# Two-layer decoder trunk on one core: queries in reversed order without the copied bias table, scores of two heads in one 128-row matmul over zero-padded keys, value products alternating between heads

## The chip, the cores and the metric

The kernel runs on one core of one Trainium2 chip. The metric is device time in microseconds (us) for one execution. TensorE (PE) does the matmuls, VectorE (DVE) and ScalarE (ACT) do elementwise work and empty the accumulator memory (PSUM), GpSimd (POOL) does elementwise work in SBUF, and SyncE (SP) issues most of the DMAs. Each engine works through its own list of instructions in order and waits for others by semaphores.

## The reference, cut to what matters

The trunk has two layers. Layer 0 runs Mamba-2 heads (SSM) and attention heads beside each other and joins them in one output projection. Layer 1 is a convolution module. Each layer ends with a gated feed-forward part (FFN). The change touches the attention: 16 key/value heads of width 64, and for each of them three queries with three patterns (window and dilation). The bias of a score depends only on the distance between query and key, through a small table.

```python
ATT_PATTERNS = ((128, 1), (512, 4), (2048, 16))

def dilated_branch(q, k, v, bias_tab, window, dil):
    ...
    delta = blk + i - j
    band = (delta >= 0) & (delta <= blk)
    ...
    bias = jnp.transpose(bias_tab[t5_bucket(jnp.maximum(delta, 0) * dil)], (2, 0, 1)).astype(jnp.float32)
    sc = jnp.einsum('bnirhd,bnjrhd->bnrhij', qb, kw).astype(jnp.float32) * (dh ** -0.5) + bias
    sc = jnp.where(mask[None, :, None, None], sc, -jnp.inf)
    m = jnp.max(sc, -1, keepdims=True)
    pr = jnp.exp(sc - m)
    l = jnp.sum(pr, -1, keepdims=True)
    o = jnp.einsum('bnrhij,bnjrhd->bnirhd', (pr / l).astype(v.dtype), vw)
    ...
```

The three patterns of a head are then joined with weights from a softmax over their log-sums. There are 512 tokens.

## The kernel before

All activations lie feature-major (features on the 128 partitions, the 512 tokens along the free axis). Projections with weights run as three passes in a 12-bit split of float32 (`products`, lines 206, 207 and 209): each output tile of 128x512 takes 24 matmuls. `slab` loads up to 2048 weights per partition by SP, casts them on ACT (line 193) and takes the rest on DVE (line 194). A scheduler that ran when the kernel was built placed the instructions in the engines' lists, from the dependences, the buffers of the pools and a cost model; so the order of the source isn't the order of an engine.

The stages that matter here:

- **SSM, four groups.** `ssm_inputs` makes the inputs of a group by `products` (tiles `bc`, `x`, `z`). `ssm_group` walks four chunks of 128 tokens. For each chunk SP loads `ar` (line 485: 512 KB, rows of `a_dram` spread over all partitions) and, from the second chunk on, `ef` (line 512, two DMAs). POOL subtracts in `ar` (486), DVE clips it (487), ACT takes the exponential (488), DVE multiplies by the mask `cb` (498, 499), and PE forms `pd` (503: weights of 64 columns, so a head fills half of the array's columns, and the heads of a chunk take the halves in turn), `po` (515) and `pst` (525). The tiles `ef` and `xde` have two buffers each, and `draw` and `arow` share one.
- **The bias.** Ahead of the groups the bias of all distances is computed into `bv` and written to `b_dram` (16 heads x 896 floats, 56 KB). Four DMAs (line 563) then copy it 128 times over into `b_rep`, 7 MB in DRAM. For the scores of a pair of heads, three DMAs (line 691) fetch `bt` (128 queries x 2 heads x 512 keys) from `b_rep`: partition i reads copy i, and starts i elements earlier than partition 0, since a query one later is one farther from each key. That is the step `LTOT - 1` in the access pattern.
- **Attention, eight pairs of heads.** `att_inputs` makes keys and three queries for two heads at a time (tiles `kq`, `qq`), 64 partitions for each head, and values (`v`, lines 645 to 648) for each second pair. `att_pair` takes one head after the other (`for e in range(2)`): 12 score matmuls over 64 rows, 128 or 256 keys wide (line 707), each emptied by one DVE instruction that adds the bias and takes the maximum (708); exponentials on ACT (732); 11 transposes (745) whose copies are `pt`. After both heads come the 22 value products (lines 788 to 793) with weights of 64 columns, all of head 0 ahead of those of head 1 in the source. The weights of the three patterns go through DRAM (`s_dram`, `w_dram`) and come back as `at`. The outputs of two pairs enter the output projection (`mixed_chunk`); with `y_chunk` and the next pair's `products` it is the work that PE has beside the chain of a pair. Keys `k0` and queries `q0` of the natural order lie in one buffer for even pairs and another for odd ones; `k1`, `q1`, `q2` in the order by token modulo 4 have one buffer.
- **FFN, convolution, FFN, final norm** follow.

Of the kernel before, what the change touches and what calls it, by code (L numbers as in the profile page):

```python
# [9 lines left out]
F32 = mybir.dt.float32  # L10
# [3 lines left out]
ALU = mybir.AluOpType  # L14
# [32 lines left out]
def shape_constants():  # L47
    """Identity, triangle and the buckets of the distances: from shapes alone."""
# [28 lines left out]
def trunk_kernel(ctx: ExitStack, tc, a, out, dbg=None):  # L77
# [14 lines left out]
    # ---------------------------------------------------------------- constants and parameters  # L92
# [7 lines left out]
    def rows(specs, name, col=None):  # L100
        """Vectors as rows of 128, transposed to a column for each row."""
# [16 lines left out]
    def ada_load(pool, l, j0, q, bufs):  # L118
        """Half slabs of ada_w, four chunks of columns wide."""
# [26 lines left out]
    # ---------------------------------------------------------------- adaLN vectors  # L146
# [50 lines left out]
    def products(w, offs, acts, name, tag="pj", cols=ALL, outs=None):  # L197
        """A bank for each list of weight offsets; acts are (hi, lo) pairs."""
# [29 lines left out]
    class Stat:  # L228
        """Sum over features of the squares, for each token of cols."""
# [36 lines left out]
    def spread(v, nb, name):  # L266
        """v [tokens of a block, block] to a bank that holds it in each partition."""
# [13 lines left out]
    class Norm:  # L281
        """h = x * rstd * g * (1 + sc) + sh, feature-major, in two parts."""
# [71 lines left out]
    # ---------------------------------------------------------------- the other parameters  # L354
# [20 lines left out]
    # ---------------------------------------------------------------- SSM  # L375
# [11 lines left out]
    draw = ssm.tile([HEADS, T], F32, tag="draw", name="draw", bufs=1)  # L387
# [44 lines left out]
    arow = ssm.tile([HEADS, T], F32, tag="draw", name="arow", bufs=1)  # L432
# [44 lines left out]
    def ssm_group(g, bt, ct, xs, zs):  # L477
        y1 = ssm.tile([P, 4, T], F32, tag="y1", name=f"y1_{g}", bufs=1)
        prev = None
        for c in range(NB):  # L480
# [37 lines left out]
            if c < NB - 1:  # L518
# [3 lines left out]
                xde = ssm.tile([P, HPG, 64], F32, tag="xde", name="xde" + n)  # L522
# [38 lines left out]
    b_rep = dram.tile([16, P * LTOT], F32, name="b_rep")  # L561
    for q in range(4):
        nc.sync.dma_start(b_rep[4 * q:4 * q + 4, :].rearrange("h (i u) -> h i u", u=LTOT),  # L563
                          b_dram[4 * q:4 * q + 4, :].unsqueeze(1).broadcast_to([4, P, LTOT]))

# [14 lines left out]
    # ---------------------------------------------------------------- attention  # L580
# [7 lines left out]
    SB = "ABABCCCAB"  # L588
# [12 lines left out]
    def out_chunk(rows_, acts, name, last=None, after=None):  # L601
        """Four tiles of wout's rows, by the heads' outputs."""
# [31 lines left out]
    def values(hp):  # L634
        """The values of two pairs of heads, token-major in both orders of the tokens."""
# [18 lines left out]

    def att_inputs(hp, vs):
        def cols(o):
            return (win[:, o + hp * P:o + (hp + 1) * P], KT, P)
# [5 lines left out]
        def nat(tag, ps, scale):  # L663
            t = (att if hp % 2 else early).tile([P, T], F32, tag=tag, name=tag + n, bufs=1)
            S.mul(t, ps, scale) if scale != 1.0 else S.copy(t, ps)
            r[tag] = t

        def mod4(tag, ps, scale):
            t = early.tile([P, 4, P], F32, tag=tag, name=tag + n, bufs=1)
            src = ps.rearrange("p (i r) -> p r i", r=4)  # L670
            S.mul(t, src, scale) if scale != 1.0 else S.copy(t, src)
# [3 lines left out]
        nat("k0", pk, 1.0)  # L675
        mod4("k1", pk, 1.0)
# [8 lines left out]
    def att_pair(hp, r, vs):  # L685
        n = str(hp)
        bt = att.tile([P, 2, T], F32, tag="bt", name="bt" + n, bufs=1)
        bd = b_rep[2 * hp:2 * hp + 1, :]
# [438 lines left out]
```

## Time and profile before

| | us |
|---|---|
| time, median of 3 runs | 1974.75 (1972.83 to 1978.38) |
| span of the profiled execution, first to last instruction | 1970.1 |
| what lies around the span, against the median | 4.65 |
| SSM stage, about | 95 to 455 |
| attention stage, about | 455 to 965 |
| FFN, convolution module, FFN, final norm, about | 965 to 1970 |

The profile comes from one execution and names each instruction by the line of the kernel. A matmul in float32 shows as two records (two passes); the end of a matmul record is modelled, so the step from one record's start to the next one's start tells more than its length. `x8` at the end of a row of the timeline means that eight records stand together. In the tables by stretch, "busy" is the time of an engine with an instruction under way, and PEclk is the share of full speed that TensorE's clock was granted.

### The profile page before, as it was taken

The page shows a single profiled execution, that of the slowest core. Times are in us where ns is not written, and L with a number is a line of the kernel's source. Part 1 is how long each engine was busy: PE and PEld are TensorE (multiplying, and loading weights), DVE is VectorE, ACT ScalarE, POOL GpSimd, SP SyncE. Part 2 cuts the span into 40 slices and gives each one's busy share as a digit, 9 for nine tenths or more (in the row PEclk, how much of TensorE's full clock was granted, in tenths as well). Part 3 has the DMA queues.
Part 4 walks back from the last instruction along what each step waited for, and adds up shares of the span by engine and source line. Part 5 has one row for each costly group of instructions (what it writes and reads, how often), then busy time and mean ns, then how long its engine had stood idle before and what let it go on. Part 6 is the DMA issues. An engine that isn't in the chain of part 4 may idle for free.

```text
span 1970.1 us, 24711 instructions
## 1 busy us (share of the span) xinstructions
PE 1808.6 (92%) x9469; PEld 1493.7 (76%) x9469; DVE 1152.9 (59%) x2164; ACT 753.1 (38%) x1460; POOL 560.2 (28%) x486
## 2 busy tenths in 40 slices
PE   5863788999999999999899999998899999999998
PEld 3642666778687877877888888887779888888888
DVE  7714878666543545554876567348799753333336
ACT  5312323333433444333532122234777542222125
POOL 1413878352242434000300000005897510000001
PEclk8986898999999999998899999998999999999999
DMA  8426454454444444341555555333220332323224
GB/s 296 112 104 188 131 155 133 121 132 129 119 119 108 139 108 140 97 129 55 172 186 199 171 186 183 101 96 119 86 86 1 108 108 85 107 87 106 86 77 138
DMA packets 227842, 246.29 MB, mean 125 GB/s; under 512 B 11770, under 2 KB 195900, under 8 KB 227725
## 3 DMA queue, kind: packets, MB, share of 16 engines
q1 hardware_dynamic: 216589, 202.78, 33.7%
q0 software_dynamic: 11136, 41.95, 6.6%
q8 instruction: 74, 1.21, 0.3%
q14 instruction: 43, 0.35, 0.1%
HBM read 236.06 MB, written 15.98 MB: 128 GB/s over the span
## 4 chain that ended last, share of the span: by engine, by line
PE 68%; DVE 13%; DMA 6%; SPq 4%; ACT 3%; issue 3%; POOL 2%; DVEq 0%; ACTq 0%; POOLq 0%
PE fd L206 4%; PE fd L209 4%; PE fd L207 4%; PE fg L207 4%; PE fu L207 4%; PE fu L206 4%; PE fu L209 4%; PE fg L209 4%; PE fg L206 4%; PE s L707 3%; SPq L563 2%; DMA adap<-in_ada_w 2%; DVE cps L991 2%; PE wa L206 1%; PE qq L206 1%
## 5 line engine op out<-in xcount | busy, mean ns | idle before, releaser
L248 POOL TENSOR_TENSOR n_acc<-n_acc,n_q 128x256 f32<-128x256 f32 x32 | 27.5, 861 | 542.1 <-ACT n_q L244 541.9
L206 PE MATMUL fd<-uh,wd_h 128*128 128x512 f32 (+1 forms) x448 | 150.1, 351 | 0.9 <-DVE xT L596 0.9
L194 DVE TENSOR_TENSOR wf_l<-wf_w,wf_h 128x1024 fp32r<-128x1024 f32 x88 | 106.2, 1243 | 75.4 <-ACT wf_h L193 75.4
L207 PE MATMUL fd<-uh,wd_l 128*128 128x512 f32 (+1 forms) x448 | 147.8, 346 | 0.0
L193 ACT CAST wf_h<-wf_w 128x1024 fp32r<-128x1024 f32 x88 | 87.7, 1048 | 117.5 <-PE fd L209 73.4
L207 PE MATMUL fg<-n_h,wf_l 128*128 128x512 f32 x320 | 125.1, 391 | 2.0 <-DVE wf_l L194 2.0
L206 PE MATMUL fg<-n_h,wf_h 128*128 128x512 f32 x320 | 125.3, 392 | 0.7 <-ACT wf_h L193 0.5
L207 PE MATMUL fu<-n_h,wf_l 128*128 128x512 f32 x320 | 124.7, 390 | 0.0
L206 PE MATMUL fu<-n_h,wf_h 128*128 128x512 f32 x320 | 124.5, 389 | 0.0
L984 POOL TENSOR_TENSOR cv<-cv,pr 128x256 f32<-128x256 f32 x150 | 114.8, 795 | 15.1 <-ACT pr L983 13.0
L732 ACT ACTIVATE s<-s,nm 128x128 f32<-128x128 f32 x192 | 79.6, 416 | 83.8 <-DVE nm L728 53.9
L171 POOL TENSOR_TENSOR adap<-adap 128x512 f32<-128x512 f32 (+2 forms) x96 | 101.7, 1065 | 4.3
L862 DVE TENSOR_TENSOR fs<-fs,fu 128x512 f32<-128x512 f32 x40 | 27.5, 688 | 127.8 <-PE fu L209 127.8
L596 DVE SCALAR_TENSOR_TENSOR xT<-fd,mod,xT 128x512 f32<-128x512 f32 (+1 forms) x64 | 39.1, 616 | 101.5 <-PE fd L209 101.2
L193 ACT CAST wd_h<-wd_w 128x1024 fp32r<-128x1024 f32 (+1 forms) x64 | 57.1, 940 | 103.0 <-PE fd L209 82.8
L206 PEld LDWEIGHTS fd<-uh,wd_h 128*128 128x128 f32 x448 | 84.3, 188 | 13.2 <-DVE xT L596 1.3
L209 PE MATMUL fd<-ul,wd_h 128*128 128x512 f32 (+1 forms) x448 | 93.1, 346 | 0.0
L207 PEld LDWEIGHTS fd<-uh,wd_l 128*128 128x128 f32 x448 | 84.3, 188 | 11.0
L169 POOL TENSOR_TENSOR adap<-adap,cs 128x1024 f32<-128x1024 f32 x32 | 65.5, 2050 | 87.3 <-DMA adap<-in_ada_w 87.3
L194 DVE TENSOR_TENSOR wd_l<-wd_w,wd_h 128x1024 fp32r<-128x1024 f32 (+1 forms) x64 | 67.7, 1091 | 35.1 <-ACT wd_h L193 34.8
L991 DVE SCALAR_TENSOR_TENSOR cps<-cu,taps,cps 128x256 f32<-128x256 f32 x203 | 87.2, 481 | 1.5
L161 DVE SCALAR_TENSOR_TENSOR adaa<-adaw,cs,adaa 128x512 f32<-128x512 f32 x112 | 84.9, 758 | 2.6
(422 smaller groups left out, 4972.5 us busy)
## 6 DMA issues: line engine op xcount, KB each, us to landing
adaw<-in_ada_w POOLq DMA_DIRECT2D x24, 1024.0 KB, 5.7
wf_w<-in_ffn_w_gate SPq DMA_DIRECT2D x22, 1024.0 KB
wf_w<-in_ffn_w_up SPq DMA_DIRECT2D x22, 1024.0 KB
adap<-in_ada_w POOLq DMA_DIRECT2D x32, 512.0 KB, 5.9
wd_w<-in_ffn_w_down SPq DMA_DIRECT2D x16, 1024.0 KB
wd_w<-in_ffn_w_down SPq DMA_DIRECT2D x16, 768.0 KB
wa_w<-in_hy_w_out SPq DMA_DIRECT2D x20, 512.0 KB
adaw<-in_ada_w SPq DMA_DIRECT2D x8, 1024.0 KB
```

The source lines that it names most:

```text
L161: V.scalar_tensor_tensor(acc, ws[k // 4][:, k % 4, :], cs[:, k:k + 1], acc, op0=ALU.mult, op1=ALU.add)
L169: G.tensor_tensor(w3, w3, cs.unsqueeze(2).broadcast_to([P, KT, P]), op=ALU.mult)
L171: G.tensor_tensor(w[:, 0:n], w[:, 0:n], w[:, n:2 * n], op=ALU.add)
L193: S.copy(hi[:, s:e], raw[:, s:e])
L194: eng.tensor_tensor(lo[:, s:e], raw[:, s:e], hi[:, s:e].bitcast(F32), op=ALU.subtract)
L206: PE.matmul(ps[:, cols], hi[:, o(k):o(k) + P], xh, start=k == 0, stop=False)
L207: PE.matmul(ps[:, cols], lo[:, o(k):o(k) + P], xh, start=False, stop=False)
L209: PE.matmul(ps[:, cols], hi[:, o(k):o(k) + P], acts[k][1][:, cols], start=False, stop=k == nk - 1)
L707: marks[hp, e] = PE.matmul(ps[:, o:o + wd], q, k, start=True, stop=True)
L732: S.activation(s[:, o:o + wd], s[:, o:o + wd], AF.Exp, bias=nm, accum_out=l)
L984: G.tensor_tensor(o, o, pr, op=ALU.add)
L991: V.scalar_tensor_tensor(o if t == TAPS - 1 else ps, tap(us[k], t), tapw(t, k), ps, op0=ALU.mult, op1=ALU.add)
```

## The change

1. **Bias.** `b_rep` and its four DMAs go. Queries are written in reversed order inside each block of 128 (`[:, :, ::-1]` in `nat` and `mod4`), so partition i is query 127 - i, and partition i reads its bias one element later than partition 0: `bt` comes straight from `b_dram` with step 1. The outputs are reversed back where they are split in two parts (`at[:, ::-1]`). The loads `bt` keep their sizes.
2. **Scores.** Keys go to `kz0` and `kz1`, which hold for each of the two heads a copy whose other 64 partitions are zero. These two tiles have one buffer each for the whole stage, are zeroed once by four memsets, and are filled for each pair by four ACT copies of 64 partitions in place of two of 128. One matmul of 128 rows with the two heads' keys side by side gives both heads' scores: 12 matmuls of 256 or 512 columns for a pair in place of 24 of 128 or 256. DVE empties each by two instructions, one for each head, of the same widths as before. All scores of both heads come ahead of the first head's exponentials in the source. `q0` has one buffer too.
3. **Value products.** The loop over heads is now the innermost one, so that neighbours write to different halves of the array's columns.
4. **Buffers.** To make room, `draw`, `arow`, `ef` and `xde` of the SSM stage share one pool of three buffers (`xe`) in place of five.

```diff
-    b_rep = dram.tile([16, P * LTOT], F32, name="b_rep")
-    for q in range(4):
-        nc.sync.dma_start(b_rep[4 * q:4 * q + 4, :].rearrange("h (i u) -> h i u", u=LTOT),
-                          b_dram[4 * q:4 * q + 4, :].unsqueeze(1).broadcast_to([4, P, LTOT]))
...
-                ef = ssm.tile([P, 4, P], F32, tag="ef", name="ef" + n)
+                ef = ssm.tile([P, 4, P], F32, tag="xe", name="ef" + n, bufs=3)
...
-                xde = ssm.tile([P, HPG, 64], F32, tag="xde", name="xde" + n)
+                xde = ssm.tile([P, HPG, 64], F32, tag="xe", name="xde" + n, bufs=3)
...
+    kz0 = early.tile([P, 2, T], F32, tag="kz0", name="kz0", bufs=1)
+    kz1 = early.tile([P, 2, 4, P], F32, tag="kz1", name="kz1", bufs=1)
+    for t in [kz0, kz1.rearrange("p e r i -> p e (r i)")]:
+        V.memset(t[64:128, 0, :], 0.0)
+        V.memset(t[0:64, 1, :], 0.0)
...
-            t = (att if hp % 2 else early).tile([P, T], F32, tag=tag, name=tag + n, bufs=1)
-            S.mul(t, ps, scale) if scale != 1.0 else S.copy(t, ps)
+            t = early.tile([P, T], F32, tag=tag, name=tag + n, bufs=1)
+            if scale != 1.0:
+                S.mul(t.rearrange("p (b i) -> p b i", b=NB), ps.rearrange("p (b i) -> p b i", b=NB)[:, :, ::-1], scale)
...
-        nat("k0", pk, 1.0)
-        mod4("k1", pk, 1.0)
+        for e in range(2):
+            hs = slice(e * 64, (e + 1) * 64)
+            S.copy(kz0[hs, e, :], pk[hs, :])
+            S.copy(kz1[hs, e, :, :], pk[hs, :].rearrange("p (i r) -> p r i", r=4))
...
-            src = bass.AP(tensor=bd.tensor, offset=bd.offset + OB[g] + 127, ap=[[LTOT - 1, P], [P * LTOT, 2], [1, wd]])
+            src = bass.AP(tensor=bd.tensor, offset=bd.offset + OB[g], ap=[[1, P], [LTOT, 2], [1, wd]])
...
+        def score(tag, name, jobs):
+            ps, o = bank(tag, name), 0
+            for q, k, bo, wd, dst, m, b in jobs:
+                marks[hp, 0] = marks[hp, 1] = PE.matmul(ps[:, o:o + 2 * wd].rearrange("p (e w) -> p e w", e=2), q, k,
+                                                        start=True, stop=True)
+                for e in range(2):
+                    V.tensor_tensor_reduce(ss[e][:, dst:dst + wd], ps[:, o + e * wd:o + (e + 1) * wd],
+                                           bt[:, e, bo:bo + wd], 1.0, -3e38, op0=ALU.add, op1=ALU.max,
+                                           accum_out=m[:, 3 - b, e:e + 1])
+                o += 2 * wd
...
+            for b in range(4):
+                ks = [(v1, b, 896 + b * P)] if j else [(v0, b, 2 * b * P)] if b == 0 else \
+                    [(v0, b - 1, (2 * b - 1) * P), (v0, b, 2 * b * P)]
+                for i, (v, kb, po) in enumerate(ks):
+                    for e in range(2):
+                        fs = slice((hp % 2) * P + e * 64, (hp % 2) * P + (e + 1) * 64)
+                        PE.matmul(ps[e * 64:(e + 1) * 64, (3 - b) * P:(4 - b) * P], v[:, kb, fs], pts[e][:, po:po + P],
+                                  start=i == 0, stop=i == len(ks) - 1)
...
-        S.copy(ah, at)
-        V.tensor_tensor(aL, at, ah.bitcast(F32), op=ALU.subtract)
+        S.copy(ah, at[:, ::-1])
+        V.tensor_tensor(aL, at[:, ::-1], ah.bitcast(F32), op=ALU.subtract)
```

Three places in the engines' lists show what the scheduler made of it. The first is SP, behind the first SSM inputs: `b_dram` is the written bias, `ar_1` (buffer numbers behind the name) the second chunk's `ar`, `wx` and `wz` the next group's weights. Before:

```order
L485 DMA ar_0_849<-a_dram 128x8x128
L560 DMA b_dram<-bv 16x896
L563 DMA b_rep<-b_dram 512x1x896 x4
L485 DMA ar_1_885<-a_dram 128x8x128
L185 DMA wx_0_w<-in_hy_w_in 128x8x256
L185 DMA wx_1_w<-in_hy_w_in 128x8x256
L485 DMA ar_2_932<-a_dram 128x8x128
```

and in the change:

```order
L485 DMA ar_0_844<-a_dram 128x8x128
L560 DMA b_dram<-bv 16x896
L485 DMA ar_1_880<-a_dram 128x8x128
L185 DMA wx_0_w<-in_hy_w_in 128x8x256
L185 DMA wx_1_w<-in_hy_w_in 128x8x256
L512 DMA ef_1_907<-a_dram 64x4x128 x2
L485 DMA ar_2_927<-a_dram 128x8x128
L512 DMA ef_2_954<-a_dram 64x4x128 x2
```

The four copies are gone from between `b_dram` and the second `ar`, and the loads `ef_1` and `ef_2`, which stood together some rows ahead of this place, now stand behind the weights and behind `ar_2`.

The second place is PE at the first pair's value products; `o` is their bank, `pt_0` and `pt_1` are the two heads' transposed probabilities, `qq` the next pair's queries. Before:

```order
L745 MATMUL pt_1_1_3223<-cst,s_1_3171 128x128 x3
L790 MATMUL o_3261<-pt_1_3216,v_0_2993 64x128
L745 MATMUL pt_1_2_3228<-cst,s_1_3171 128x128 x4
L792 MATMUL o_3261<-pt_1_3216,v_0_2993 64x128
L793 MATMUL o_3261<-pt_1_3216,v_0_2993 64x128
L792 MATMUL o_3261<-pt_1_3216,v_0_2993 64x128
L788 MATMUL o_3277<-pt_0_3153,v_0_2994 64x128 x4
```

and in the change:

```order
L755 MATMUL pt_1_2_3217<-cst,s_1_3110 128x128 x4
L798 MATMUL o_3250<-pt_1_3205,v_0_2994 64x128
L798 MATMUL o_3250<-pt_0_3171,v_0_2994 64x128
L798 MATMUL o_3250<-pt_1_3205,v_0_2994 64x128
L798 MATMUL o_3250<-pt_0_3171,v_0_2994 64x128
L798 MATMUL o_3250<-pt_1_3205,v_0_2994 64x128
```

Products of the two heads now follow each other in turn. Of the 176 value products of all pairs, 142 stand directly behind another one, and in 135 of these the other one is of the other head; before, neighbours were of the same head but for 8 places. The 96 score matmuls of the change stand in 52 groups between other matmuls, the 192 before in 83.

The third place is ACT, at the exponentials of the first pair (`s`, two heads) and the copies of the second pair's queries (`q`) and keys out of the banks `kq`. Before:

```order
L732 ACTIVATE s_0_3108,st_3107<-s_0_3108,nm_3106 128x128
L732 ACTIVATE s_0_3108,l_3104<-s_0_3108,nm_3106 128x128
L665 ACTIVATE q_3385<-kq_1_3332 128x512
L193 CAST wa_h<-wa_w 128x1024 x2
L671 COPY k_3383<-kq_0_3331 128x512
```

and in the change:

```order
L742 ACTIVATE s_1_3110,st_3108<-s_1_3110,nm_3107 128x128
L742 ACTIVATE s_1_3110,l_3105<-s_1_3110,nm_3107 128x128
L668 ACTIVATE q_3374<-kq_1_3321 128x512
L193 CAST wa_h<-wa_w 128x1024 x2
L676 ACTIVATE q_3435<-qq_0_3385 128x512
```

Before, the copy of `q` stood behind the eight exponentials of head 0; now it stands behind sixteen, eight of each head, and the four copies of the keys stand ahead of these.

More of the change, by code (lines that the diff above doesn't have):

```diff
@@ L587, in trunk_kernel @@
     YB, Y4, MX = 4, {5: (8, None), 7: (12, (7, 1))}, {}
-    SB = "ABABCCCAB"
+    SB = "    CCCAB"
     ry = att.tile([P, T], F32, tag="ry", name="ry", bufs=1)
@@ L699, in att_pair, with blk @@
         m1, l1 = st[:, :, 0:2], st[:, :, 2:4]
+        ss = [att.tile([P, 1920], F32, tag="s", name=f"s{n}_{e}") for e in range(2)]
+        def blk(b):
+            return slice(b * P, (b + 1) * P)
+        def score(tag, name, jobs):
[8 more added lines that the diff above has]
+                o += 2 * wd
@@ new lines, in att_pair @@
+        q0, k0 = r["q0"], kz0
+        score("A", f"s0{n}", [(q0[:, blk(0)], k0[:, :, blk(0)], 128, P, 0, m0, 0)])
+        for b in (1, 2, 3):
+            score("BAB"[b - 1], f"s0{n}_{b}",
+                  [(q0[:, blk(b)], k0[:, :, (b - 1) * P:(b + 1) * P], 0, 256, 128 + (b - 1) * 256, m0, b)])
+        for g, m in ((1, m1), (2, m2)):
+            for i in range(2):
+                score("AB"[i], f"s{g}{n}_{i}",
+                      [(r[f"q{g}"][:, b, :], kz1[:, :, b, :], 128 + g * P, P, 384 + g * 512 + b * P, m, b)
+                       for b in (2 * i, 2 * i + 1)])
@@ L700, in att_pair @@
         pts = []
         for e in range(2):
-            hs = slice(e * 64, (e + 1) * 64)
-            s = att.tile([P, 1920], F32, tag="s", name=f"s{n}_{e}")
-            def score(ps, o, q, k, bias, dst, m):
-                wd = bias.shape[-1]
-                marks[hp, e] = PE.matmul(ps[:, o:o + wd], q, k, start=True, stop=True)
-                V.tensor_tensor_reduce(s[:, dst:dst + wd], ps[:, o:o + wd], bias, 1.0, -3e38,
-                                       op0=ALU.add, op1=ALU.max, accum_out=m)
@@ L722, in att_pair @@
-            for g, m in ((1, m1), (2, m2)):
-                ps = bank(SB[g + 1], f"s{g + 1}{n}_{e}")
-                for b in range(4):
-                    score(ps, b * P, r[f"q{g}"][hs, b, :], r["k1"][hs, b, :], bt[:, e, 128 + g * P:256 + g * P],
-                          384 + g * 512 + b * P, m[:, b, e:e + 1])
+            s = ss[e]
             V.tensor_tensor(m1[:, :, e], m1[:, :, e], m2[:, :, e], op=ALU.max)
@@ L781, in att_pair @@
             ps = bank(SB[7 + j], f"o{j}{n}")
-            for e in range(2):
-                pt = pts[e]
-                fs = slice((hp % 2) * P + e * 64, (hp % 2) * P + (e + 1) * 64)
-                for b in range(4):
-                    o = ps[e * 64:(e + 1) * 64, b * P:(b + 1) * P]
-                    if j:
-                        PE.matmul(o, v1[:, b, fs], pt[:, 896 + b * P:896 + (b + 1) * P], start=True, stop=True)
-                    elif b == 0:
-                        PE.matmul(o, v0[:, 0, fs], pt[:, 0:P], start=True, stop=True)
-                    else:
-                        PE.matmul(o, v0[:, b - 1, fs], pt[:, (2 * b - 1) * P:2 * b * P], start=True, stop=False)
-                        PE.matmul(o, v0[:, b, fs], pt[:, 2 * b * P:(2 * b + 1) * P], start=False, stop=True)
+            for b in range(4):
[6 more added lines that the diff above has]
+                                  start=i == 0, stop=i == len(ks) - 1)
             if j:
```

28 lines of the change are left out of this document (10 added, 18 removed).

## The prediction

> **What bounds the kernel now.** I read the page first: how busy each engine is, its slices, and the chain of work that ended last.
>
> ```profile
> span 1970.1 us, 24711 instructions
> PE 1808.6 (92%) x9469; PEld 1493.7 (76%) x9469; DVE 1152.9 (59%) x2164; ACT 753.1 (38%) x1460; POOL 560.2 (28%) x486
> PE   5863788999999999999899999998899999999998
> PE 68%; DVE 13%; DMA 6%; SPq 4%; ACT 3%; issue 3%; POOL 2%; DVEq 0%; ACTq 0%; POOLq 0%
> ```
>
> PE is busy 92% of the span, and most of the chain is PE. A slice is 49 us; the fourth (148 to 197 us) has a 3, in the middle of the SSM stage. And 4% of the chain is SP's own queue, which is odd for an engine that only issues transfers. So I looked at the engines by stretch (PE, PEld, DVE, ACT, POOL busy us, then clock, DMA share, GB/s; the last row is the attention stage):
>
> ```profile
> 110.00:125.00 15.00, 15.00 (x81) 11.89 (x80) 3.12 (x6) 2.09 (x5) 4.09 (x4) 1.00 0.26 105
> 125.00:140.00 15.00, 3.10 (x14) 2.00 (x12) 0.00 (x0) 0.00 (x0) 0.00 (x0) 0.75 0.26 105
> 140.00:155.00 15.00, 0.00 (x0) 0.00 (x0) 0.00 (x0) 0.00 (x0) 0.00 (x0) 0.50 0.26 105
> 170.00:185.00 15.00, 10.15 (x49) 7.79 (x50) 9.37 (x12) 6.57 (x9) 5.75 (x4) 0.66 0.83 240
> 185.00:200.00 15.00, 11.41 (x59) 8.85 (x59) 15.00 (x23) 4.21 (x6) 10.32 (x7) 0.89 0.76 211
> 200.00:220.00 20.00, 15.96 (x87) 12.66 (x85) 18.83 (x18) 8.27 (x11) 15.73 (x11) 1.00 0.51 125
> ...
> 455.00:965.00 510.00, 501.74 (x2693) 396.00 (x2693) 268.80 (x799) 211.19 (x588) 126.89 (x105) 0.97 0.41 117
> ```
>
> From about 128 to 173 us no compute engine works at all. In the attention stage PE is busy for 502 of 510 us and DVE for little more than half. What stops the machine is in the waits from 95 to 180 us (total, times, longest) and in SP's timeline (start, duration):
>
> ```profile
> POOL ar L486 <- DMA ar<-a_dram: 57.7, 2, 52.0
> DVE ar L487 <- POOL ar L486: 57.1, 2, 55.3
> PE pb L519 <- DVE cb L498: 46.8, 1, 46.8
> ...
> 97.25 42.65 SPq L563 DMA_DIRECT2D b_rep<-b_dram  x4
> ...
> 169.66 2.40 SPq L485 DMA_DIRECT2D ar<-a_dram  x1
> ```
>
> SP spends 42.65 us issuing the four copies of the bias, and the loads behind them take as long as the copies drain. POOL waits 52 us for the second `ar`, DVE for POOL, PE for DVE. So the change has two different places to work on: a stall of the whole machine, and a stage bound by PE.
>
> **The copies go (term A).** Without them the second `ar` follows `b_dram`, at about 97 us. A later load of this kind shows on the chain as
>
> ```profile
> 203.12 4.94 DMA ar<-a_dram
> ```
>
> so POOL has it at about 102 and not at 172. PE had its own work until about 128, so its wait of 46.8 us goes. In the chain 72 us lie between the first copy's issue (97.25) and 169.66; that is the most that can go. For what comes after the stall, DVE is the bound: it is busy 15.00 of 15 us and 18.83 of 20 between 185 and 220, while in 110 to 125 it had 3.12 of 15. It can now start that backlog some 25 us ahead of PE, so a part of PE's idle time of 3.6 and 4.0 us in these two stretches goes, and of the slow clock (0.66 in 170 to 185, so PE's 10.15 us there are worth some 7). I take 47 + 3 for the clock + 6, **A = -56**, between -44 (some of the wait comes back) and -72. The loads `bt` keep their sizes and their places in SP's list; their other source costs nothing that a row here shows.
>
> **Value products (term B).** Here are three neighbours of one head (488.76 to 489.25), and eight matmuls of line 503, which have the same shape but change halves at each matmul, with their successors:
>
> ```profile
> 488.76 0.43 PE L790 MATMUL o<-pt,v 128*64 128x128 f32 x2
> 489.03 0.38 PE L792 MATMUL o<-pt,v 128*64 128x128 f32 x2
> 489.25 0.38 PE L793 MATMUL o<-pt,v 128*64 128x128 f32 x2
> ...
> 115.04 1.09 PE L503 MATMUL pd<-ar,xdt 128*64 128x128 f32 x16
> 116.06 1.12 PE L525 MATMUL pst<-xde,btok 128*128 128x512 f32 x2
> 117.02 0.38 PE L496 MATMUL pb<-sc,sb 128*128 128x128 f32 x2
> ```
>
> From start to start one product of one head takes 0.22 us; of line 503 eight take 1.02, so 0.13 each. There are 8 x 22 = 176 products: 176 x (0.22 - 0.13) = 16, **B = -16**, between 0 (the heads don't overlap) and -22.
>
> **Scores (term C).** The columns that stream through the array don't change: for a pair 2 x (9 x 128 + 3 x 256) = 3840 before, 9 x 256 + 3 x 512 = 3840 now. What can go is what a change between 64 and 128 rows costs. All scores of the attention stage (PE busy, then PEld), one of them between products, and from the chain eight products in a run and 14 float32 records of 256 columns and 128 rows:
>
> ```profile
> 465.00:960.00 495.00, 76.83 (x384) 51.82 (x384) 0.97 0.41 117
> ...
> 480.89 0.47 PE L206 MATMUL kq<-n_h,wa_h 128*128 128x512 f32 x1
> 481.29 0.48 PE L707 MATMUL s<-k,q 64*128 64x128 f32 x2
> 481.71 0.50 PE L207 MATMUL kq<-n_h,wa_l 128*128 128x512 f32 x1
> 482.05 0.39 PE L206 MATMUL kq<-n_h,wa_h 128*128 128x512 f32 x1
> ...
> 553.37 1.81 PE qq L209 x8
> ...
> 1509.58 3.02 PE cps L1006 x14
> ```
>
> The score takes 0.42 us from start to start, and its two neighbours 0.40 and 0.34, where a product in a run takes 1.81 / 8 = 0.23. With 128 rows a record of 256 columns takes 3.02 / 14 = 0.216 us and one of 512 about 0.48 (116.06 to 117.02, two). A pair then costs 18 x 0.216 + 6 x 0.48 = 6.8 us, eight pairs 54. With 5 us of waits for emptied banks that is 59 against 76.8 of busy time, and some 0.1 us less at the start of a good half of the 83 groups: **C = -22**, between 0 (rival 2) and -33.
>
> [...]
>
> **What it adds.** The memsets stand on DVE between two rows with idle time between them (the bracket is idle time before the row):
>
> ```profile
> 49.08 0.10 DVE L552 MEMSET tab<- 1x48 f32 x1
> 53.20 0.29 DVE L402 TENSOR_TENSOR dt_v<-dt_t,dtb 128x128 f32<-128x128 f32 x1 [4.03 <-PE dt_t L391]
> ```
>
> `ones`, 128 elements wide, takes 0.17 us; four of 512 at the same rate take 2.6, less than 4.03: 0, and 2.6 if that idle time were gone. The three buffers in place of five make each `ef` wait for an earlier `xde` or `ef`. ACT, in order, waited for `ef` already, and SP for its buffer (SSM stage, 200 to 460 us):
>
> ```profile
> ACT ef L513 <- DMA ef<-a_dram: 45.4, 9, 13.7
> SPq L512 <- DVE y L516: 17.8, 6, 6.3
> ```
>
> A wait is 5 us in the mean. ACT's other work hid most of it, as PE is busy for 15.96 of 20 us in the stretch from 200 on. If all nine loads came a wait later and nothing hid it, that were 45; if the scheduler's new places suit, 0. I take +5, nearer to the hidden case. The second queue is ACT's in attention: `q` now stands behind sixteen exponentials and all its banks wait; PE has 24 to 48 products between. I take +3, at most 12 (1.5 for each pair).
>
> **Sum.** -56 - 16 - 22 + 5 + 3 = -86. Against the profiled execution (1970.1 of span, 4.65 below the median of 1974.75) the span would be 1884; I keep the 4.65 around it: 1974.75 - 86 = **1889 us**.
>
> **The rivals.**
>
> 1. *The stall refills.* The second `ar` comes at once, but `ef_2` and `ef_3` now wait for `pst` of two chunks before, and DVE, which waits for them in `y`, holds up the weights' split. For it: DVE is full right behind the stall. Against it: 15 us windows in which DVE does 3. Then A is -44 and the buffers +15: 1974.75 - 44 - 16 - 22 + 15 + 3 = 1911.
>
> 2. *DVE sets the pace of the scores.* It empties them in the same pieces as before:
>
> ```profile
> L708 DVE CUSTOM_DVE_ANT_0 s<-s,bt 128x128 f32<-128x128 f32 x144 | 38.2, 287 | 45.1 <-PE s L707 35.6 <-issue 3.9 <-PE pt L745 3.4
> L708 DVE CUSTOM_DVE_ANT_0 s<-s,bt 128x256 f32<-128x256 f32 x48 | 19.4, 419 | 6.5 <-PE s L707 6.2
> L708 DVE DVE_READ_ACCUMULATOR2_ANT m<- 128x1 f32 x128 | 10.5, 82 | 0.0
> ```
>
> Each piece is followed by a read of 82 ns: 144 x 0.369 + 48 x 0.501 = 77 us, what the scores take on PE today. For it: in the last pair 11 score matmuls stand together. Against it: in most others products stand between them, 52 groups in all. Then C is 0: 1911. [...]
>
> 3. *Slower: one buffer of keys and ACT's order.* The next pair's keys must wait for the last score of this pair, and their banks hold up the next products; in the change ACT has up to 24 exponentials in that place.
>
> ```profile
> L732 ACT ACTIVATE s<-s,nm 128x128 f32<-128x128 f32 x144 | 55.9, 390 | 83.8 <-DVE nm L728 53.9 <-DVE nm L729 29.9
> L732 ACT ACTIVATION_READ_ACCUMULATOR s<-s,nm 128x1 f32 x192 | 36.1, 188 | 0.0
> L671 ACT COPY k<-kq 128x512 f32<-128x512 f32 x8 | 4.7, 582 | 0.4 <-PE s L707 0.4
> ```
>
> 24 x (0.39 + 0.19) + 4 x 0.58 = 16.2 us a pair; if PE waited all of it each time, +130 and 2019. It decides from 86 / 8 = 10.8 us of PE wait a pair. Against it: `k1` had one buffer before too and waited 0.4 us, and ACT is busy for 211 of 510 us.
>
> 4. *More of it works:* A -72, B -20, C -28 and +5: 1860.
>
> That the change doesn't do what it says is excluded for the order (the rows above show it), and a part of rivals 1 and 2 otherwise.
>
> **How the numbers follow.** Forecast 0.55; rival 1 0.17; rival 2 0.15; rival 4 0.09; rival 3 0.04. The range of 1855 to 1925 takes in rivals 1, 2 and 4 and their mixtures, as the unknown costs (+45 and +12) reach it in part. All cases but rival 3 are faster by over 0.3% (5.9 us, about what a measurement can tell from no change): 0.95 after rounding; rival 3 and the worst mixtures leave 0.02 for within 0.3% and 0.03 for slower.
>
> **What the profile after would show.** A: no stretch from 95 to 200 us without compute, and DVE's 55 us wait gone; wrong if PE still waits there for over 10 us. B: value products some 0.13 us from start to start. C: neighbours of a score at 0.23 us, and PE's busy time of the scores near 59; at 77, rival 2. Buffers: ACT's wait for `ef` no more than 45 us. ACT's order: PE's waits in attention below 10 us in all. The prediction is wrong if PE's time in attention doesn't fall, or if the SSM stage gives back over 20 us of the stall.

## The result and the profile after

The changed kernel takes **1890.0 us** (median of 4 runs, 1884.0 to 1896.6) against 1974.3 us (4 runs, 1972.8 to 1978.4): a ratio of 0.958, 95% interval 0.955 to 0.962, 84 us less. Run again later beside other kernels it had a ratio of 0.956 (0.954 to 0.959). The profiled execution has a span of 1894.8 us and took 1896.6 us, the longest of its four. From its page, the lines that answer to those of before:

```profile
span 1894.8 us, 24381 instructions
PE 1770.6 (93%) x9277; PEld 1475.4 (78%) x9277; DVE 1150.2 (61%) x2168; ACT 761.5 (40%) x1476; POOL 564.4 (30%) x486
PE   5897979999999999989999999979899899999998
PE 73%; DVE 11%; DMA 6%; ACT 4%; issue 3%; POOL 2%; SPq 0%; DVEq 0%; POOLq 0%; ACTq 0%
```

The 3 in PE's fourth slice is a 7, and SP's queue has left the chain (4% before). The stretches of the SSM stage, and the attention stage as a whole (PE, PEld, DVE, ACT, POOL busy us, clock, DMA share, GB/s):

```profile
125.00:140.00 15.00, 14.06 (x94) 10.74 (x93) 9.89 (x13) 3.31 (x6) 7.29 (x6) 1.00 0.48 132
140.00:155.00 15.00, 10.67 (x42) 8.38 (x41) 12.20 (x15) 6.49 (x8) 9.96 (x7) 0.89 0.50 132
155.00:170.00 15.00, 14.43 (x81) 11.53 (x79) 14.24 (x18) 4.56 (x6) 9.40 (x6) 1.00 0.58 163
170.00:185.00 15.00, 6.75 (x22) 5.25 (x23) 14.96 (x16) 7.01 (x11) 15.00 (x11) 0.66 0.29 94
...
417.00:876.00 459.00, 442.87 (x2416) 357.15 (x2415) 264.70 (x789) 214.34 (x596) 128.21 (x104) 0.99 0.44 128
```

No stretch is without compute now. But from 170 to 185 us PE works for 6.75 us only, while DVE (14.96) and POOL (15.00) are full: part of the stall comes back as a backlog of those two. The waits of 95 to 180 us (total, times, longest):

```profile
ACT ar L488 <- DVE ar L487: 23.8, 5, 10.6
ACT ef L513 <- DMA ef<-a_dram: 12.5, 2, 7.8
POOL ar L486 <- DMA ar<-a_dram: 10.7, 4, 4.6
...
PE pb L519 <- DVE cb L498: 5.7, 1, 5.7
```

POOL's wait for `ar`, 57.7 us before, is 10.7, and PE's for `cb`, 46.8 before, is 5.7. In the attention stage, all scores of 410 to 875 us (PE busy, PEld), and pieces of PE's timeline:

```profile
410.00:875.00 465.00, 62.01 (x192) 34.83 (x192) 0.99 0.44 128
...
427.42 0.59 PE L716 MATMUL s<-kz,q 128*128 128x256 f32 x2
427.67 0.58 PE L206 MATMUL kq<-n_h,wa_h 128*128 128x512 f32 x1
428.09 0.59 PE L716 MATMUL s<-kz,q 128*128 128x256 f32 x2
428.33 0.58 PE L207 MATMUL kq<-n_h,wa_l 128*128 128x512 f32 x1
```

A score of both heads takes 0.25 us from start to start, where one of a single head took 0.42. The product behind it takes 0.42, more than the 0.34 that it took behind a score of one head, and not the 0.23 of a product in a run. The value products of the two heads, where they stand together (nine matmuls of two records each):

```profile
548.11 1.31 PE L798 MATMUL o<-pt,v 128*64 128x128 f32 x18
```

That is 0.15 us a product with the end of the last one, where one of a single head took 0.22 to 0.27.

Where the 75 us went between the two profiled spans, by the first score, the last product `wa` and the first product of the convolution module: up to the first score 467.5 to 417.2, so -50; the attention stage 497.4 to 458.6, so -39; the FFN -2.5; and from there on 16 us come back, nearly all in the convolution module, whose code the change doesn't touch.

**How the rest is counted.** PE is the bound of the attention stage, so its length is split in three: time in which PE is idle; time lost because the clock was granted at half (half of PE's busy time in such stretches of the trace's record of the clock, an estimate: a product record of 512 columns at L209 follows the last one after 227 ns at full clock and 427 ns at half, medians of before and of after alike); and the rest, called work. Before: 497.4 = 8.3 idle + 13.7 lost + 475.5 work. After: 458.6 = 16.1 + 2.7 + 439.8. So the work fell by 36, the loss by 11, and the idle time grew by 8.

### The profile page after: what moved, and what is told of

Read it like the earlier page. It is cut to its first block, busy times and chain, and to the rows that moved or that the text cites. A ratio compares the mean times of both kernels' runs of the same rounds, so it can differ in the third digit from the quotient of the medians.

```text
span 1894.8 us, 24381 instructions
## 1 busy us (share of the span) xinstructions
PE 1770.6 (93%) x9277; PEld 1475.4 (78%) x9277; DVE 1150.2 (61%) x2168; ACT 761.5 (40%) x1476; POOL 564.4 (30%) x486
## 4 chain that ended last, share of the span: by engine, by line
PE 73%; DVE 11%; DMA 6%; ACT 4%; issue 3%; POOL 2%; SPq 0%; DVEq 0%; POOLq 0%; ACTq 0%
PE fd L206 4%; PE fd L209 4%; PE fd L207 4%; PE fg L207 4%; PE fg L206 4%; PE fu L206 4%; PE fu L207 4%; PE fu L209 4%; PE fg L209 4%; PE cps L1012 2%; DMA ar<-a_dram 1%; PE s L716 1%; PE z L206 1%; PE z L207 1%; PE qq L206 1%
## 5 line engine op out<-in xcount | busy, mean ns | idle before, releaser
L171 POOL TENSOR_TENSOR adap<-adap 128x128 f32<-128x128 f32 (+2 forms) x96 | 104.6, 1094 | 4.7
L209 PE MATMUL fd<-ul,wd_h 128*128 128x512 f32 (+1 forms) x448 | 93.2, 346 | 0.0
L194 DVE TENSOR_TENSOR wd_l<-wd_w,wd_h 128x1024 fp32r<-128x1024 f32 (+1 forms) x64 | 67.7, 1090 | 34.9 <-ACT wd_h L193 34.8
```

The lines of the kernel that those rows point to most:

```text
L171: G.tensor_tensor(w[:, 0:n], w[:, 0:n], w[:, n:2 * n], op=ALU.add)
L194: eng.tensor_tensor(lo[:, s:e], raw[:, s:e], hi[:, s:e].bitcast(F32), op=ALU.subtract)
L209: PE.matmul(ps[:, cols], hi[:, o(k):o(k) + P], acts[k][1][:, cols], start=False, stop=k == nk - 1)
```

## The experiments

Each kernel was timed in five rounds beside the kernel before. The table gives the ratio to it, the SSM stage from 90 us on, and the split of the attention stage (first score to last product `wa`) from each profile. Differences in us to the kernel before are to the executions beside it, whose median lay between 1969.4 and 1974.3.

| run | median us | ratio (95%) | SSM to first score, PE idle in it | attention = idle + lost + work |
|---|---|---|---|---|
| before | 1974.3 | 1 | 377.5, 82.6 | 497.4 = 8.3 + 13.7 + 475.5 |
| after | 1890.0 | 0.958 (0.955-0.962) | 327.2, 35.0 | 458.6 = 16.1 + 2.7 + 439.8 |
| e12_after | 1884.6 | 0.956 (0.954-0.959) | 324.4, 32.0 | 454.6 = 13.0 + 3.7 + 437.8 |
| e1_rev | 1925.8 | 0.978 (0.976-0.980) | 325.8, 33.0 | 492.9 = 8.4 + 9.7 + 474.8 |
| e2_rev_xe | 1913.5 | 0.972 (0.970-0.974) | 322.4, 31.2 | 494.5 = 6.4 + 13.6 + 474.5 |
| e7_copies | 1946.4 | 0.989 (0.987-0.991) | 384.7, 91.3 | 457.2 = 15.2 + 2.2 + 439.7 |
| e10_spread | 1953.6 | 0.991 (0.989-0.993) | 363.2, 66.5 | 489.1 = 7.7 + 6.6 + 474.9 |
| e3_alt | 1960.2 | 0.995 (0.994-0.997) | 377.7, 83.3 | 481.0 = 10.5 + 11.3 + 459.3 |
| e4_headwise | 1893.8 | 0.960 (0.958-0.963) | 320.9, 32.4 | 463.7 = 11.4 + 1.4 + 450.9 |
| e5_rows64 | 1917.4 | 0.973 (0.971-0.975) | 324.0, 31.7 | 493.1 = 13.9 + 17.1 + 462.1 |
| e6_pad1 | 1888.2 | 0.958 (0.956-0.960) | 323.5, 33.6 | 466.1 = 20.0 + 8.1 + 438.0 |
| e8_rowtiles | 1891.2 | 0.958 (0.956-0.960) | 329.5, 34.8 | 460.3 = 18.6 + 13.7 + 428.0 |
| e9_rows_alt | 1892.9 | 0.959 (0.957-0.961) | 325.5, 33.9 | 470.2 = 28.3 + 17.5 + 424.4 |
| e13_tail | 1886.0 | 0.958 (0.955-0.960) | 322.0, 32.8 | 453.7 = 12.5 + 1.6 + 439.6 |

**e1_rev: the copies alone.** The kernel before with the reversed queries and no `b_rep`.

```
-    b_rep = dram.tile([16, P * LTOT], F32, name="b_rep")
-    for q in range(4):
-        nc.sync.dma_start(b_rep[4 * q:4 * q + 4, :].rearrange("h (i u) -> h i u", u=LTOT),
-                          b_dram[4 * q:4 * q + 4, :].unsqueeze(1).broadcast_to([4, P, LTOT]))
...
-            S.mul(t, src, scale) if scale != 1.0 else S.copy(t, src)
+            S.mul(t, src[:, :, ::-1], scale) if scale != 1.0 else S.copy(t, src)
...
-        bd = b_rep[2 * hp:2 * hp + 1, :]
+        bd = b_dram[2 * hp:2 * hp + 1, :]
```

> The kernel before with the reversed queries alone: the four copies b_rep<-b_dram are gone and bt is read straight from b_dram; five SSM buffers, scores on 64 rows and value products head by head stay as before. Theory (term A by itself, -56): 1974 - 56 = 1918 us, with no stretch from 95 to 200 us without compute, and the attention stage (first score to last out product) unchanged at 497 us. Rival 1 (the stall refills): -44, 1930 us, and DVE or POOL full for 30 us or more right behind 140 us. Rival 4: -72, 1902 us. Rival 5 (the reversed reads on ACT and DVE and the new order of the pieces cost something): the attention stage grows by more than 3 us.

Measured: 43.6 us less. The stage up to the first score is 51.7 us shorter, with 49.6 us less of PE idle. The windows (columns as above):

```profile
140.00:155.00 15.00, 12.89 (x72) 10.00 (x71) 14.24 (x21) 6.18 (x8) 11.62 (x8) 1.00 0.56 168
155.00:170.00 15.00, 8.79 (x40) 6.69 (x38) 15.00 (x16) 3.65 (x6) 13.69 (x10) 0.86 0.46 123
170.00:185.00 15.00, 10.30 (x33) 8.02 (x34) 13.93 (x13) 5.77 (x10) 11.84 (x9) 0.73 0.57 175
```

DVE is full where the stall was, as rival 1 had it. Yet most of the gap between 52 and 44 arises elsewhere: by the profiles the convolution module is 9 us longer than before, 10 us more of it lost at half clock. Rival 5 falls: the attention stage is 4.5 us shorter, not longer.

**e7_copies: the copies put back into the kernel after, and nothing reads them.**

```
     nc.sync.dma_start(b_dram, bv)
+    b_rep = dram.tile([16, P * LTOT], F32, name="b_rep")
+    for q in range(4):
+        nc.sync.dma_start(b_rep[4 * q:4 * q + 4, :].rearrange("h (i u) -> h i u", u=LTOT),
+                          b_dram[4 * q:4 * q + 4, :].unsqueeze(1).broadcast_to([4, P, LTOT]))
```

> The kernel after with the four copies into b_rep put back where they stood; nothing reads them, so only SP's issue and the transfers come back. Theory (term A is the copies in SP's queue, whoever reads them): +56 on 1890, so 1946 us, with the stretch without compute back at some 128 to 173 us and POOL waiting about 50 us for the second ar. Rival 1 (a part of the stall comes back anyway in the kernel after, as POOL is full in 170 to 185 us): +44 or less, 1934 us. Rival 6 (what made the stall was the readers of b_rep, not the copies): no change, 1890 us.

Measured: 0.989 against 0.956 to 0.958, some 60 us more. The longest waits of the stall are back to within a microsecond, in the waits of 95 to 200 us and in SP's timeline:

```profile
POOL ar L486 <- DMA ar<-a_dram: 62.7, 3, 52.6
...
PE pb L519 <- DVE cb L498: 47.1, 1, 47.1
...
97.03 43.12 SPq L563 DMA_DIRECT2D b_rep<-b_dram  x4
```

So the copies make the stall, whoever reads them; rival 6 falls.

**e10_spread: the same copies, one at a time.** The kernel before, each copy behind the `ef` loads of one SSM group.

```
         ssm_group(g, *ins)
+        with tc.issue_after(marks["ef"].ins):
+            nc.sync.dma_start(b_rep[4 * g:4 * g + 4, :].rearrange("h (i u) -> h i u", u=LTOT),
+                              b_dram[4 * g:4 * g + 4, :].unsqueeze(1).broadcast_to([4, P, LTOT]))
```

> The kernel before with the four copies kept and read, but each issued on SP behind the ef loads of one SSM group instead of all four together ahead of the second ar. Theory (what stalls is the place in SP's queue: 47 us of loads behind four copies in a row): four holds of 47 / 4 = 12 us, of which the loads behind them hide a part, so 20 to 44 us of the 44 that e1_rev gained: 1927 to 1950 us, with no window of 15 us without compute. Rival 10 (the amount counts, wherever it stands): 1970 us, four stalls of 12 us each on PE.

Measured: 18 us less than before by the ratio (20 by the medians), so some 0.4 of what e1_rev gains: just short of what the theory gave it, and not the "no change" of rival 10. In SP's timeline and the waits of 95 to 455 us:

```profile
133.37 0.69 SPq L565 DMA_DIRECT2D b_rep<-b_dram  x1
136.03 7.55 SPq L485 DMA_DIRECT2D ar<-a_dram  x1
143.69 9.74 SPq L512 DMA_DIRECT2D ef<-a_dram  x2
...
POOL ar L486 <- DMA ar<-a_dram: 89.1, 8, 27.4
ACT ef L513 <- DMA ef<-a_dram: 82.7, 9, 19.6
```

The issue of a single copy holds SP for 0.69 us only, where the four in a row held it for 42.65. But the next loads then hold it: 7.55 and 9.74 us here, where such loads take 0.37 and 1.24 ahead of that copy. That is some 17 us behind one copy, about a quarter of the 72 us between the first copy's issue (97.25) and the third `ar`'s (169.66) before. And the loads come late, up to 27.4 us for `ar`. The kernel before shows the same: the copies' packets, of 3584 bytes, run from 97 to 169 us (105 GB/s from 110 to 155), the issue of the second `ar` takes 17.76 us at 139.94, and its first packets start at 158 us. That the transfers in front of a load make its issue long fits this, but was not shown by itself: two loads `wx` take 13.84 us to issue at 99.23 in e10_spread, ahead of the first copy. Spreading hides only part of the cost (18 to 20 of the 43.6 us): both the place and the amount count.

**e2_rev_xe: three SSM buffers.** e1_rev and, alike for `draw`, `arow` and `xde`:

```
-                ef = ssm.tile([P, 4, P], F32, tag="ef", name="ef" + n)
+                ef = ssm.tile([P, 4, P], F32, tag="xe", name="ef" + n, bufs=3)
```

> The run e1_rev and one thing more: draw, arow, ef and xde share three buffers instead of five. Theory (term xe, +5): 5 us above e1_rev, some 1923 us. If the scheduler's new places suit: 0. Rival 1 (nothing hides the wait): up to +15, and at most +45 over e1_rev, with ACT's wait for the DMA of ef above 45 us. The attention stage must not change by this edit.

Measured: 12 us less than e1_rev, not 5 more. ACT's waits for `ef`, from 95 us to the first score, sum to 39.7 us against 41.4. In the profiles, 7.0 us apart, the SSM stage is 3.4 us shorter and the last part of the convolution module 4.6, where PE's order of instructions differs between the two kernels though the code doesn't: e2_rev_xe has the order of the kernel before there, e1_rev another one. By the mean granted clock of all executions (0.974 and 0.970) at most 8 of the 12 us are the clock's. That the buffers of one stage move the scheduler's order in another was seen, not explained.

**e3_alt and e4_headwise: the value products alone, and undone.** In the first the loop over the heads goes innermost in the kernel before; in the second it goes outermost again in the kernel after.

```
-            for e in range(2):
-                for b in range(4):
+            for b in range(4):
...
+                for i, (v, kb, po) in enumerate(ks):
+                    for e in range(2):
```

> The kernel before with the value products alone alternating between the two heads; copies, buffers and scores as before. Theory (term B, -16): 1958 us, value products at 0.13 us from start to start or below where they stand together. If the halves of the array don't run side by side: 0, 1974 us. At most -22: 1952 us.

> The kernel after with the value products head by head again (all eleven of one head, then all of the other, each bank), the rest as after. Theory (term B, 16 us): 1890 + 16 = 1906 us, PE's start-to-start time of the value products back at 0.12 to 0.2 us. If the gain of the alternation is hidden elsewhere: 1890 us.

Measured: alone 9 us less than before; undone 4 to 8 us more than after, hardly more than the noise (the intervals of 0.960 and 0.958 overlap). On PE the edit is worth what was foretold: the 176 products take 44.4 us from start to start in the kernel before, 28.3 in e3_alt, 27.7 after and 41.0 in e4_headwise; the work falls by 16.2 in e3_alt and rises by 11 to 13 in e4_headwise. In e4_headwise less idle time and less loss cover much of it (12.8 us of both against 18.8 and 16.7 after). In e3_alt nothing covers it: the attention stage is shorter by 16.4 us, with idle and lost time as before (21.8 and 22.0 us). There a part of the gain is given back behind the stage: from the first product of the convolution module on, the profile is 5 us longer than before, with 7.6 us more lost at half clock in that module. The rest of the gap between 16 and 9 is open.

**e5_rows64 and e6_pad1: the scores.** In the first the score loop of before on the new key buffers, with 64 rows and one head after the other, so the order of the exponentials is the one of before too; in the second the padded matmul cut in two, which is the diff shown.

```
-                marks[hp, 0] = marks[hp, 1] = PE.matmul(ps[:, o:o + 2 * wd].rearrange("p (e w) -> p e w", e=2), q, k,
-                                                        start=True, stop=True)
+                for e in range(2):
+                    marks[hp, 0] = marks[hp, 1] = PE.matmul(ps[:, o + e * wd:o + (e + 1) * wd], q, k[:, e],
+                                                            start=True, stop=True)
```

> The kernel after with the score part as before: one matmul of 64 rows for each head and piece, head after head, with the banks, the maxima and the exponentials in that order; the padded key buffers stay allocated and filled, so copies, buffers and value products are as after. Theory (term C, 22 us, and 3 us back for the exponentials' order): 1890 + 19 = 1909 us; by the starts in the trace of after (scores 27 us less than before) up to 1917 us. Rival 2 (DVE paces the scores, C = 0): 1890 us.

> The kernel after with each padded score matmul cut into two of 128 rows, one for each head (384 in place of 192, all with 128 rows, same columns). Theory (what C saves is the change between 64 and 128 rows, not the number of matmuls): no more than 3 us from the kernel after, 1890 us. Rival 7 (the number of score matmuls, or of their weight loads, is what costs): half or more of the 22 us comes back, 1901 us or more.

Measured: e5_rows64 takes 27 to 33 us more than after, e6_pad1 the same as after. PE's busy time of the scores in the attention stage, of e5_rows64 and of e6_pad1:

```profile
414.00:907.00 493.00, 77.18 (x384) 51.63 (x384) 0.96 0.41 119
```

```profile
413.00:880.00 467.00, 62.12 (x384) 55.53 (x384) 0.98 0.44 126
```

The same number of records, the same columns: 77.2 us with 64 rows, 62.1 with 128. So the rows make it, not the number; rivals 2 and 7 fall. Against the second profile of after, e5_rows64 has 24 us more work, 13 us more lost at half clock and 1 us more idle. The 27 to 33 us are those of the rows and of ACT's order together; no run has 64 rows one after the other with the order of after.

**e8_rowtiles and e9_rows_alt: the opposite of padding.** 64 rows, the two heads in different banks, so that they can run side by side; in e9_rows_alt PE's order is fixed to strict alternation, and the SSM buffers are shared (the diff is that of e9_rows_alt; e8_rowtiles has no `issue_after` and `e` in 0, 1).

```
+            ps = [bank("AB"[e], f"{name}_{e}") for e in range(2)]
...
             for q, k, bo, wd, dst, m, b in jobs:
...
+                for e in (1, 0):
+                    hs = slice(e * 64, (e + 1) * 64)
+                    with tc.issue_after(last.ins) if last else nullcontext():
+                        last = PE.matmul(ps[e][:, o:o + wd], q[hs], k[hs], start=True, stop=True)
```

> The run e1_rev with alternating value products, and the scores on 64 rows with the two heads issued in turn into two different banks, so that they could run side by side on the two halves of the rows; five SSM buffers, no padded keys. Theory (a change of rows costs some 0.3 us a group, and two row halves do run side by side): scores 26 us of streaming and 12 to 25 us for the changes, against 49 from start to start in the kernel after, and 5 us less for the buffers: 1874 to 1887 us. Rival 8 (they don't run side by side): 51 us of streaming and the same changes, 1899 to 1912 us.

> The run e8_rowtiles with two things more: PE's order of the scores is fixed to head 1, head 0, head 1, head 0 within a piece (in e8 three of one head often stand together, and the median from start to start is 105 ns where two side by side would make 112 ns for both), and the three shared SSM buffers as in the kernel after. Theory (the two row halves run side by side when they alternate; what is left is the 0.17 us by which the next matmul starts late after a 64-row one): streaming 37 us in e8 falls to 26, with some 40 to 60 changes at 0.2 to 0.3 us the scores take 36 to 42 us from start to start in place of 51, and SSM as in e2_rev_xe 3 to 10 us less than in e1_rev: 1865 to 1880 us. Rival 9 (the alternation makes PE wait for two banks at once, and idle time takes the place): 1885 to 1895 us.

Measured: both as fast as after, not faster, so neither came down to the times of its theory. The 0.2 to 0.3 us for a change of rows in the two theories were estimates; what the traces show behind a score of 64 rows stands at term C below. Side by side the heads do run: e9_rows_alt's scores keep PE busy for

```profile
415.00:886.00 471.00, 42.82 (x384) 30.95 (x384) 0.96 0.42 122
```

42.8 us against 77.2, and the stage has 13 us less work than the second profile of after. But it is 16 us longer: 15 us more idle and 14 us more lost. Its waits of PE in that stage:

```profile
PE wa L206 <- ACT ath L804: 8.0, 2, 4.7
PE ada L152 <- POOL adap L171: 4.6, 2, 2.5
PE pt L750 <- DVE mod L154: 4.2, 1, 4.2
PE s L711 <- DVE m L717: 3.8, 4, 1.8
PE pt L750 <- POOL s L745: 3.1, 1, 3.1
```

They are on three engines, so there is no single next bound: `ath`, `pt` and `s` belong to a pair's own chain, `ada` and `mod` to the vectors of the adaptive norms, which are made on the side. That the products which used to cover a pair's softmax now run out before it is done is what the waits suggest; no run tests it. The time is rival 9's, and idle time takes the gain's place as it said, but the wait that it named, for the banks of the scores, is 3.8 us where it was 3.3 and 3.2 after.

**e12_after: the kernel after once more.**

> The kernel after itself, once more, beside the two others on the same chip. 0.9583 of the kernel before: 1889 us. In its profile the part of the convolution module from the first mu product to the last pq product took 106 us against 96 before; if that is a chance of the granted clock it varies between 96 and 106 from profile to profile with the same program, if it is the scheduler's other order there it stays 4 us or more above 96.

Measured: 0.956 of the kernel before. The convolution module's last part takes 98.7 us, 1.8 lost at half clock, where the first profile of the same program had 105.9 and 11.9. So of the 10 us by which it was longer than before, 7 are a chance of the clock, and some 3 stay in this profile; PE's order there is not that of the kernel before, and its idle time is 9.1 against 5.7. The other traces bear the order out: the six kernels with the order of the kernel before in that part (before, e2_rev_xe, e6_pad1, e8_rowtiles, e9_rows_alt, e13_tail) take 96 to 98 us for it, the four profiles with the order of after 99 to 106, the others 99 to 103. Such an order comes out of the scheduler and was in no term of the prediction.

**e13_tail: an attempt to fill the last wait.** Of the last output chunk, the products of the two SSM tiles are put ahead.

```
-    mixed_chunk(3, acts[6:], nrm)
+    out_chunk([(3 * 2 * P, 2)], y_tiles(6, 2), "wt3", after=marks[7, 1])
+    out_chunk([(DI + 3 * 2 * P, 2)], acts[6:], "wa3", nrm)
```

> The kernel after with the last out products in two parts: the 48 products of the two SSM tiles stand ahead, where PE waits 4.6 us for the last pair's ath (the rest of the last chunk follows). In the kernel after the clock is granted at half for 6.8 us right behind that wait, which costs another 3.4 us. Theory (a wait of PE costs its own length and the clock behind it): 8 us less than the kernel after, 0.957 of the kernel before less 8 us: some 1878 us. Rival 11 (the clock loss is a chance and not the wait's): 4.6 us less, 1882 us. Rival 12 (the residuals twice over the same tiles, or another wait, take its place): no change, 1887 us.

Measured: 0.958, no change. The wait for `ath` is gone, and behind the shorter last chunk the norm is not ready:

```profile
PE n_b L273 <- DVE n_d L270: 11.4, 1, 11.4
```

Rival 12. No version of these beats the kernel after.

## Why the prediction came out as it did

The forecast of 1889 us was met to 1 us, but by terms whose errors cancel: that it came so close is luck.

- **A, the copies (-56).** The mechanism is shown: put back, they cost some 60 us; taken out alone, the SSM stage loses 51.7 of its 377.5 us, against the 56 foretold. In time 43.6 remain, which is rival 1's number, but not by its mechanism alone: the part named there (DVE full behind the stall) is seen, yet most of the step from 52 to 44 lies in the convolution module. One sign failed: in the kernel after PE waits for 14 us between 125 and 185 us, more than the 10 that the prediction set as its limit. The term was too large by what I didn't count: the backlog in 140 to 185 us, and the losses later in the program.
- **Buffers (+5).** The sign was wrong: -12 in the medians, with -3.4 in the SSM stage. The step that failed is that fewer buffers were to lengthen ACT's wait for `ef`: from 95 us to the first score it was 45.4 us before, 41.4 in e1_rev with five buffers, and 39.7 in e2_rev_xe with three, and PE's nine longest waits of the stage name `ef` in none of the three. Where the 12 us come from is open but for the 4.6 us of the convolution module.
- **B, value products (-16).** On PE right: 0.25 us a product before, 0.16 after (44.4 and 27.7 us over 176), as against 0.22 and 0.13 in the sum, which took the shorter one of the two steps in its rows (0.27 and 0.22). In time it is -9 alone, and 4 to 8 when undone. The step that failed is the equation of PE's work with time, and not in one way: in e3_alt the stage gained all of it, and 5 us came back behind the stage; in e4_headwise idle and lost time changed with the work. And e5_rows64, which has the alternation on top of e2_rev_xe, is no faster than that (0.973 and 0.972): 12 us less work, 11 us more idle and lost time. It has the padded key buffers and their copies on ACT as well, so this is not the alternation's doing alone.
- **C, scores (-22).** The busy time was put at 59 and is 62; rival 2's 77 is excluded. As work on PE it is 22 to 24 us, as foretold. As time it is larger: 27 to 33 us by e5_rows64, which undoes ACT's order with it (19 expected), since the sum left out the clock, 13 us in that profile. One sign failed: the product behind a score takes 0.42 us and not 0.23. What goes is the 0.17 us at the score itself, and half of the pieces, since a piece now serves two heads. In the traces, behind a score of 64 rows and 128 columns the next other matmul starts 202 ns after the start of the score's last record, behind one of 128 rows and 256 columns after 28 ns (medians of the stage, before and after). What the array does in between, no trace shows.
- **The reverse of this change.** Two row halves side by side bring the scores on PE from 77.2 us of busy time to 42.8 (e5_rows64 and e9_rows_alt), and against 64 rows one head after the other the time falls too (0.973 and 0.959); but it is no faster than padding (0.956 to 0.958). Of e9_rows_alt's 28 us of idle time 3.8 us are waits for emptied scores, the others are spread.
- **ACT's order (+3).** PE's idle time in the attention stage grew by 5 to 8 us, within the bounds. But the place is another: `q` behind the exponentials costs 1.2 us at `qq` and 0.9 at `v`; the largest wait is the last pair's `ath`, 4.5 us. "Below 10 us in all" was missed by both profiles (16.1 and 13.0). Rival 3 would have needed 86 us.
- **The sum.** The parts tried alone make -56 (e2_rev_xe), -9 and, with the others present, -27 to -33: -92 to -98, where the whole gives -84 to -89. The parts overlap by 3 to 14 us, which is little more than the noise of three such differences; where a part lost something (e4_headwise, e5_rows64), it went into waits, half clock and the scheduler's order of other stages.

## What to carry to other kernels

In a stage where one engine is busy for 98%, a saving on it can shorten the stage by its full price (e3_alt: 16 of 16 us) or come back as waits and half clock (e9_rows_alt: 13 us less work, 29 us more of both). So ask what work of the other engines the saved work had covered. A bulk copy between two DRAM tensors on the queue that feeds the next stage was paid by the loads behind it (POOL waited 52.0 us for `ar`), also when it was spread (27.4 us) and when nothing read it (52.6 us). A changed kernel can get another order in a stage that wasn't touched: compare that stage too before a term is given its price. When a prediction comes out right, undo its parts one by one all the same: four terms of this one were off by 5 to 17 us and cancelled.

## What the runs showed of the hardware

In the traces of before and after the clock is granted at full or at half (1.0 or 0.5), in stretches of 3.41 us or multiples (at half 3.41 to 47.8 us), but for those that the end of a run cuts. In the attention stages of before and after, each half stretch begins behind 3.4 us in which PE was busy for 85% or less (85, 32 and 71% before, 0% after). Two places, the last pair's scores before, and the wait for `ath` after (columns as above):

```profile
886.80:890.20 3.40, 3.40 (x17) 2.63 (x16) 2.07 (x4) 1.12 (x3) 0.00 (x0) 1.00 0.00 0
890.20:893.70 3.50, 2.50 (x17) 2.13 (x16) 3.33 (x16) 1.98 (x3) 0.00 (x0) 1.00 0.01 2
893.70:897.10 3.40, 3.40 (x11) 1.95 (x10) 2.86 (x15) 1.72 (x7) 0.00 (x0) 0.51 0.22 34
897.10:910.70 13.60, 13.60 (x48) 10.10 (x48) 4.64 (x30) 7.78 (x37) 1.26 (x1) 0.50 0.18 70
```

```profile
844.40:847.80 3.40, 0.00 (x0) 0.00 (x0) 3.40 (x6) 0.14 (x1) 0.00 (x0) 1.00 0.74 277
847.80:854.60 6.80, 5.31 (x23) 5.02 (x24) 2.32 (x5) 2.40 (x6) 0.73 (x1) 0.50 0.47 154
```

Before, 1 us of idle in the last pair's scores is followed by 17 us at half clock, which cost 8.5 us by the estimate above. That place goes with the rows: the six versions with scores of 64 rows one head after the other (before, e1_rev, e2_rev_xe, e3_alt, e5_rows64, e10_spread) have 10 to 20 us at half clock there, the two with row halves side by side 3 to 7, the six with 128 rows none. This is a part of what term C gained in time.

What sets off a half stretch is open. A lower busy share of PE isn't enough: the attention stage after has ten stretches of 3.4 us with PE busy for 54 to 81% and full clock behind them, the first rows below. Nor is a busy PE a full guard: further on in the same profile half clock follows 3.4 us with PE busy throughout, mostly with matmuls of one column (the ends of their records are modelled, so that share may be too high).

```profile
697.60:701.00 3.40, 1.83 (x12) 1.17 (x11) 0.17 (x1) 3.38 (x16) 1.60 (x2) 1.00 0.00 0
701.00:704.40 3.40, 3.40 (x15) 2.78 (x16) 2.60 (x5) 3.15 (x5) 0.53 (x1) 1.00 0.11 5
...
1411.00:1414.40 3.40, 3.40 (x28) 3.27 (x28) 3.40 (x10) 2.70 (x8) 3.08 (x6) 1.00 0.02 5
1414.40:1421.20 6.80, 6.80 (x23) 5.81 (x23) 5.98 (x18) 4.41 (x9) 6.17 (x9) 0.50 0.00 0
```

The length of PE's gaps doesn't settle it either: the half stretch in the attention stage after begins 3.5 us into the longest gap, the 4.55 us of the wait for `ath`, but those of the attention stage before came with no gap above 2.3 us. Behind the wait for `ath` PE was busy for 5.31 us at half clock, so some 2.7 us were lost by the estimate above; that the wait set it off was not shown. How much is lost varies: the same program lost 11.9 and 1.8 us in the same part of the convolution module in two profiles.
